# A two-layer decoder trunk on one core: half of the last output projection by seven block products instead of eight, and the last scan begun sooner

## The chip, the cores and the metric

The kernel runs on one core of a Trainium2 chip. The metric is the device time of one execution in microseconds; before the change the median of 3 runs is 2236.33 us (2235.79 to 2238.73). Lower is better.

## The reference

One sequence of 512 tokens, 2048 channels, two residual layers in f32: layer 0 is gated differential attention, layer 1 gated RWKV-7 time mixing. The change concerns layer 1, and there the last scan and the output projection:

```python
D_MODEL = 2048
SEQ = 512
DEPTH = 2

def wkv7_scan(r, w, k, v, a, b):
    ...
    def step(S, inp):
        r_t, w_t, k_t, v_t, a_t, b_t = inp
        sa = jnp.einsum('bhvk,bhk->bhv', S, a_t)
        S = S * w_t[:, :, None, :] + sa[..., None] * b_t[:, :, None, :] + v_t[..., None] * k_t[:, :, None, :]
        y = jnp.einsum('bhvk,bhk->bhv', S, r_t)
        return S, y

def rwkv7_mixer(...):
    ...
    y = wkv7_scan(rh, heads(decay), kh, vh, -kk, kk * ah)
    mean = jnp.mean(y, axis=-1, keepdims=True)
    var = jnp.mean(jnp.square(y - mean), axis=-1, keepdims=True)
    y = (y - mean) * lax.rsqrt(var + GN_EPS)
    y = y * gn_w.astype(F32).reshape(RW_HEADS, RW_HEAD_DIM) + gn_b.astype(F32).reshape(RW_HEADS, RW_HEAD_DIM)
    y = y + jnp.sum(rh * kh * r_k.astype(F32), axis=-1, keepdims=True) * vh
    ...
```

The gated y (512 x 2048) is multiplied with w_out (2048 x 2048), and the product is added to the residual x.

## The kernel before

**Arithmetic.** Every large f32 product is made of three fast ones (`mm3`): each operand is split into a high part, rounded to the fast format (fp32r), and a low part, the rest. ACT makes the high part with a copy, DVE the low part with a subtraction; for weights `split_w` (L96, L97) does so from a raw buffer that SP's queue loads (`load_w`, L78). Buffers in SBUF: `wraw` three, `wh` two, `wl` two. The split runs with a high priority (`urgent`, AHEAD = 2000), scan steps with a higher one (SCAN = 3000): a scheduler orders each engine's instructions by priority and by when they can go, and each engine then works through its own list in that order.

**Layer 1.** It goes through 16 pairs of heads (j). For each pair come four projections of 128 channels, keys and queries, a small triangular solve on DVE (`t_solve`, ends in the store td<-Tm), which comes back through a transfer (TT<-td, issued by SP) and is turned on DVE (L874). Then a chain of small PE steps, inserted between the products of other work: `t_combine` (L880, L890), then the scan over 8 blocks of tokens with three small PE operations each (L961, L972, L979) that go through ACT, DVE and POOL, then `outputs` (L1001, L1005). `Chain` counts the products that `mm3` issues (`tick`): the three numbers in `chain(g, j, p, delay, gap, gap_s)` say how many products lie before the chain's first PE step (beginning with T's turn on DVE) and between its later ones. For the pairs 0 to 13 the gated y goes to DRAM (`yd2`, [2048, 512], channel by token); for the pairs 14 and 15 it is split in SBUF.

**The last scan.** For pair 15 nothing follows but the gate projections of pairs 13, 14 and 15 and the output projection, so its chain, with 80, 4, 4, is laid between those products. `split_rows` loads rows 0 to 13 of yd2 back and splits them; rows 14 and 15 come straight from `gated(..., True)`.

**The output projection.** Four quarters (`cb`) of 512 columns. In each, `unit_tok` goes over 8 units of two k-tiles (a unit is 256 weight rows, 512 KB) and, in each, over 4 token tiles: 2 x 4 x 3 = 24 products of 128x128 by 512 into four PSUM tiles (two `pp`, two `pt`). y is the stationary operand, the weights are streamed. In the first quarter the last unit goes k-tile by k-tile, as row 15 comes last (`all_rows`). Then for each token tile the residual row (`xr1`, loaded by SP from xd) is added on DVE (L1126) and stored through ACT's queue (L1127).

**The lines that the prediction speaks of**: L96 and L97 (split of weights), L108 (every product), L407 and L408 (split of a row of y), L874, L880, L890 (T of the solve), L1005 (end of a scan), L1125 to L1127 (residual, sum, store). The tile tags AR, G, BK, BKT, LT, VS, y, yc, r, k, th0, th1, xL, xH, E, f, l name buffers that earlier stages of layer 1 use.

Of the kernel before, what the change touches and what calls it, by code (L numbers as in the profile page):

```python
# [13 lines left out]
F32 = mybir.dt.float32  # L14
F32R = mybir.dt.float32r
# [3 lines left out]
ALU = mybir.AluOpType  # L19
# [4 lines left out]
P = 128  # L24
# [14 lines left out]
AHEAD, SCAN, SOLVE = 2000, 3000, 4000  # L39
# [45 lines left out]

@urgent
def split_w(g, parts, kg, cols, k0, raw=None, fine=False):

    nc = g.nc
    if raw is None:  # L90
        raw = g.wraw.tile([P, kg, cols], F32, name="wraw", tag="wraw")
        load_w(g, raw, parts, k0, slice(0, kg))
    hi = g.wh.tile([P, kg, cols], F32R, name="wh", tag="wh")
    lo = g.wl.tile([P, kg, cols], F32R, name="wl", tag="wl")
    for ks in [slice(k, k + 1) for k in range(kg)] if fine else [slice(0, kg)]:
        nc.scalar.copy(hi[:, ks], raw[:, ks])  # L96
        nc.vector.tensor_sub(lo[:, ks], raw[:, ks], hi[:, ks].bitcast(F32))  # L97
    return hi, lo
# [4 lines left out]
    return [(win, h * 256, 256), (win, D + h * 256, 256)]  # L103


def mm3(nc, out, aH, aL, bH, bL, start, stop, g=None):
    for a, b, s, e in ((aH, bH, start, False), (aH, bL, False, False), (aL, bH, False, stop)):
        m = nc.tensor.matmul(out, a, b, start=s, stop=e)  # L108
        if g:
            tick(g, m)  # L110
    return m
# [26 lines left out]
def tick(g, m):  # L138

    g.m = m  # L140
    if g.chains:
        c = g.chains[0]
        c.wait -= 1
        if c.wait <= 0:
            with g.tc.issue_after(m.ins):
                c.step(g)


def unit_tok(g, aH, aL, parts, cols, npp=NT, more=None):
# [473 lines left out]
@urgent  # L623
def shift_mix(g, ps, rows, mu, omu, tag, bufs=2):

    nc, w = g.nc, g.work
    o_ = w.tile([P, T], F32, name="mix" + tag, tag=tag, bufs=bufs)
    nc.scalar.activation(o_[:rows, :], ps[:rows, :], AF.Copy, scale=omu)
    nc.vector.scalar_tensor_tensor(o_[:rows, 1:], ps[:rows, 0 : T - 1], mu, o_[:rows, 1:], ALU.mult, ALU.add)  # L629
    return o_  # L630
# [310 lines left out]
def chain(g, j, p, delay, gap, gap_s, others=()):  # L941
    def steps():
        yield from t_combine(g, j, p)
        yield from scan_pair(g, j, p, gap, gap_s, dict(others))

    p.chain = Chain(g, steps(), delay)
    return p.chain
# [93 lines left out]
    nc.vector.scalar_tensor_tensor(p.y[:], ps[:], g.prm["hgw"][:, j : j + 1], p.y[:], ALU.mult, ALU.add)  # L1041


def layer1(g, aps):
    nc, tc = g.nc, g.tc
    with ExitStack() as cx:
        g.lc = cx.enter_context(tc.tile_pool(name="lc1", bufs=1))
        g.work = cx.enter_context(tc.tile_pool(name="work1", bufs=2))
        rwkv_masks(g)
        w = g.work  # L1050
        win = aps["rw_w_in"][0]
        pairs = []

        def proj(i, j, **k):
            return unit_chan(g, [(win, i * D + j * P, P)], P, **k)[0]

# [48 lines left out]
        gated(g, j - 2, pairs[j - 2], gate(g, j - 2, proj(3, j - 2)))  # L1105
        gps = proj(3, j - 1)
        group_norm(g, j - 1, pairs[j - 1])
        finish_y(g, j - 1, pairs[j - 1])
        row = gated(g, j - 1, pairs[j - 1], gate(g, j - 1, gps), True)
        gt = gate(g, j, proj(3, j))  # L1110
        rows = split_rows(g, g.yd2, ("r", "k", "th0", "th1"), 1, j - 1) + [row]

        def all_rows(n, _):
            if n >= KT and len(rows) < KT:
                group_norm(g, j, p)
                finish_y(g, j, p)
                rows.append(gated(g, j, p, gt, True))

        yH, yL = Rows(rows, 0), Rows(rows, 1)
        for cb in range(4):  # L1120
            cs = slice(cb * 512, (cb + 1) * 512)
            pts = unit_tok(g, yH, yL, [(aps["rw_w_out"][0], cb * 512, 512)], 512, 2, more=all_rows)
            for t in range(NT):
                xr = w.tile([P, 512], F32, name="xr1", tag=("r", "k", "th0", "th1")[t], bufs=1)
                nc.sync.dma_start(out=xr[:], in_=g.xd[t * P : (t + 1) * P, cs])  # L1125
                nc.vector.tensor_add(xr[:], xr[:], pts[t][:])  # L1126
# [48 lines left out]
```

## Time and profile before

| | |
|---|---|
| median of 3 runs | 2236.33 us (2235.79 to 2238.73) |
| the profiled execution | 2235.41 us |
| its span | 2233.7 us |
| DMA packets in all | 224.46 MB, mean 100 GB/s |
| end of the last scan on PE (L1005) | 2077.39 us + 0.68 |
| last product begins | 2229.34 us |

The profile is one execution. PE is the matrix engine (PEld its weight loads), DVE the vector engine, ACT the scalar engine, POOL the general one, SP the engine that issues most DMAs. A row of a group reads: line, engine, operation, tiles out<-in, shape, count, then busy us and mean ns of one, then the idle time ahead of them and what ended it. A row of a timeline reads: start, duration, engine, line, operation, and in brackets the idle time before. PE's records overlap: a product's record is 0.39 us long, and the next one begins 0.23 later. PEclk is the clock that PE was granted, 1.00 for full.

### The profile page before, as it was taken

What the parts mean: (1) busy time and instruction counts of PE and PEld (TensorE: products, weight loads), DVE (VectorE), ACT (ScalarE), POOL (GpSimd) and SP (SyncE); (2) the same over time, 40 slices, a digit from 0 to 9 for tenths busy, and PEclk for the clock granted to TensorE, in tenths of its full rate; (3) what the DMA queues carried; (4) which work ended last, traced back from release to release, by engine and by line L of the source; (5) the groups of instructions that cost most, each with busy time, mean ns of one, the idle gap of its engine ahead of it and who ended that gap; (6) DMA issues with size and microseconds to landing.
All of it is one profiled execution on the core that took longest, in us unless ns stands there. A gap on an engine that the chain in (4) does not pass through costs nothing. (4 is left out here: it accounts for less than half of the span.)

```text
span 2233.7 us, 33774 instructions
## 1 busy us (share of the span) xinstructions
PE 2184.1 (98%) x12260; PEld 1770.4 (79%) x12260; DVE 1374.9 (62%) x3666; ACT 1005.1 (45%) x2065; POOL 297.4 (13%) x672
## 2 busy tenths in 40 slices
PE   8999999999999999989999999999999999999999
PEld 6888888888888878877777777787777777777887
DVE  5555646455564664245667787777777877777322
ACT  5443434334343452225455555555455556545211
POOL 0000000000000000000323133333322233331000
PEclk9999999999999999999999999999999999999999
DMA  6222222222222254332423333333333333435333
GB/s 180 94 86 96 85 95 95 85 95 85 95 85 95 91 194 132 115 113 74 102 68 83 88 88 86 86 91 99 90 81 81 97 88 78 107 93 156 123 132 113
DMA packets 290730, 224.46 MB, mean 100 GB/s; under 512 B 47732, under 2 KB 255748, under 8 KB 290564
## 3 DMA queue, kind: packets, MB, share of 16 engines
q1 hardware_dynamic: 275892, 195.74, 30.2%
q0 software_dynamic: 6144, 10.84, 2.0%
q10 hardware_dynamic: 8528, 15.73, 2.0%
q8 instruction: 96, 1.57, 0.3%
q14 instruction: 70, 0.57, 0.1%
HBM read 202.26 MB, written 19.99 MB: 99 GB/s over the span
## 5 line engine op out<-in xcount | busy, mean ns | idle before, releaser
L97 DVE TENSOR_TENSOR wl<-wraw,wh 128x1024 fp32r<-128x1024 f32 (+2 forms) x325 | 396.0, 1219 | 498.8 <-ACT wh L96 498.2
L96 ACT CAST wh<-wraw 128x1024 fp32r<-128x1024 f32 (+2 forms) x325 | 340.0, 1046 | 659.1 <-PE pp L108 453.9
L108 PE MATMUL pp<-wh,hH 128*128 128x512 f32 x1408 | 554.7, 394 | 6.0 <-ACT hH L586 5.3
L108 PE MATMUL pp<-wh,hL 128*128 128x512 f32 x1408 | 552.6, 393 | 0.0
L108 PE MATMUL pp<-wl,hH 128*128 128x512 f32 x1408 | 552.0, 392 | 0.0
L108 PE MATMUL pp<-hL,wh 128*128 128x512 f32 (+1 forms) x1056 | 430.3, 407 | 0.1
L108 PE MATMUL pp<-hH,wl 128*128 128x512 f32 (+1 forms) x1056 | 428.3, 406 | 0.4 <-DVE wl L97 0.4
L108 PE MATMUL pp<-hH,wh 128*128 128x512 f32 (+1 forms) x1056 | 425.1, 403 | 2.1 <-DVE mixt L629 1.8
L108 PEld LDWEIGHTS pp<-wh,hH 128*128 128x128 f32 x1408 | 265.1, 188 | 60.2 <-ACT hH L586 6.0
L108 PEld LDWEIGHTS pp<-wh,hL 128*128 128x128 f32 x1408 | 265.0, 188 | 54.2 <-DVE hL L587 0.6
L108 PEld LDWEIGHTS pp<-wl,hH 128*128 128x128 f32 x1408 | 265.2, 188 | 52.3
L108 PEld LDWEIGHTS pp<-hH,wh 128*128 128x128 f32 (+1 forms) x1056 | 199.4, 189 | 40.6 <-DVE mixt L629 2.2
L108 PEld LDWEIGHTS pp<-hL,wh 128*128 128x128 f32 (+1 forms) x1056 | 199.4, 189 | 37.5 <-DVE hL L587 1.7
L108 PEld LDWEIGHTS pp<-hH,wl 128*128 128x128 f32 (+1 forms) x1056 | 199.6, 189 | 34.0 <-DVE wl L97 0.8
L850 DVE SCALAR_TENSOR_TENSOR tmpl<-LT,Tm 128x60 f32<-128x60 f32 (+24 forms) x496 | 133.1, 268 | 10.7
L967 POOL COPY SA<-VS 64x64 f32<-64x64 f32 x224 | 58.0, 259 | 445.6 <-DVE VS L983 388.1
L678 POOL MEMSET rmask<- 128x512 bf16 x1 | 0.5, 525 | 832.9 <-DVE nb L339 832.9
L852 DVE TENSOR_TENSOR Tm<-Tm,tmpl 128x60 f32<-128x60 f32 (+24 forms) x496 | 104.6, 211 | 10.9
L983 DVE SCALAR_TENSOR_TENSOR VS<-sm,gam,Sg 64x64 f32<-64x64 f32 x192 | 54.3, 283 | 51.9 <-PE sm L979 47.6
L964 ACT COPY rhs<-sm 64x64 f32<-64x64 f32 x256 | 52.6, 205 | 66.7 <-PE sm L961 64.4
L974 ACT COPY VS<-sm 64x64 f32<-64x64 f32 x256 | 52.6, 206 | 59.0 <-PE sm L972 55.2
L970 POOL TENSOR_SCALAR Sg<-SA,gam 128x64 f32<-128x64 f32 x96 | 72.1, 751 | 9.3
(269 smaller groups left out, 2801.3 us busy)
## 6 DMA issues: line engine op xcount, KB each, us to landing
wraw<-in_rw_w_in_dram SPq DMA_DIRECT2D x128, 512.0 KB, 4.0
wraw<-in_da_w_in_dram SPq DMA_DIRECT2D x254, 256.0 KB, 3.0
wraw<-in_da_w_out_dram SPq DMA_DIRECT2D x32, 512.0 KB, 3.6
wraw<-in_rw_w_out_dram SPq DMA_DIRECT2D x32, 512.0 KB, 3.6
LT<-ltd POOLq DMA_DIRECT2D x64, 132.0 KB, 2.9
yr<-yd SPq DMA_DIRECT2D x28, 256.0 KB, 3.8
xq<-in_x_dram SPq DMA_DIRECT2D x16, 256.0 KB, 5.2
xd<-xq ACTq DMA_DIRECT2D x16, 256.0 KB, 2.9
```

Source lines behind the costliest of these rows:

```text
L96: nc.scalar.copy(hi[:, ks], raw[:, ks])
L97: nc.vector.tensor_sub(lo[:, ks], raw[:, ks], hi[:, ks].bitcast(F32))
L108: m = nc.tensor.matmul(out, a, b, start=s, stop=e)
L678: nc.gpsimd.memset(g.rmask[:], 1.0)
L850: nc.vector.scalar_tensor_tensor(tt, LT[:, i : i + 1, i + 1 :].to_broadcast([P, s, n]), n2[:, i : i + 1], Tm[:, 0:s, i : i + 1].to_broadca ...
L852: nc.vector.tensor_add(Tm[:, 0:s, i + 1 :], Tm[:, 0:s, i + 1 :], tt)
L964: nc.scalar.copy(rhs[r_, :], sm[r_, h * C : h * C + C])
L967: nc.gpsimd.tensor_copy(p.SA[r_, c - 1, :], VS[r_, c, h, :])
L970: nc.gpsimd.tensor_scalar(Sg[:], p.SA[:, c - 1, :], p.gam[:, c : c + 1], None, ALU.mult)
L974: nc.scalar.copy(VS[r_, c, h, :], sm[r_, P : P + C])
L983: g.state = nc.vector.scalar_tensor_tensor(VS[r_, c + 1, h, :], s_, p.gam[r_, c : c + 1], Sg[r_, :], ALU.mult, ALU.add)
```

## The change

Three things change, all in layer 1.

1. The last scan's chain gets 24, 5, 6 in place of 80, 4, 4.
2. The first two quarters go as before. During the second, `all_sums` issues `sum_forms` four times, within units 0, 1, 3 and 5 (counted from 0): it reloads 14 rows of yd2 (k-tiles 0 to 6 and 7 to 13, in chunks of 1, 2, 2 and 2 tiles of each half) into raw buffers (`frow`, tag wraw), and makes four sums of quarter blocks (256 tokens by 7 k-tiles) on DVE, split by ACT and DVE into buffers that are free by then. The residual tiles of the second quarter use the AR buffers, two token tiles in each.
3. The last 1024 columns, two blocks c1 and c2 of 512, are made by `half_out`: y's tokens (two halves of 256), k-tiles 0 to 13 (two halves of seven) and the columns (c1, c2) form a 2x2 by 2x2 block product with the seven products of Winograd's form; k-tiles 14 and 15 are multiplied in full (`plain`). The weight sums (`comb`) are made on DVE from raw tiles, b11 is loaded twice, the outputs are gathered in f32 in four `acc` tiles that start from the residual (`take`), and stored from there.

```diff
-def mm3(nc, out, aH, aL, bH, bL, start, stop, g=None):
+def mm3(nc, out, aH, aL, bH, bL, start, stop, g=None, skip=False):
...
+NS = 7
+KS = ((0, 1), (1, 2), (3, 2), (5, 2))
+PLACES = {"11": (0, 0), "12": (0, 1), "21": (1, 0), "22": (1, 1)}
...
+def sum_forms(g, src, i):
+    nc, w = g.nc, g.work
+    k0, n = KS[i]
+    rows, out, wide = [], {}, []
+    for at in (k0, NS + k0):
+        r = g.wraw.tile([P, n, 512], F32, name="frow", tag="wraw")
+        nc.sync.dma_start(out=r[:], in_=src[at * P : (at + n) * P, :].rearrange("(k p) t -> p k t", p=P))
+        rows.append(r)
+    (a, b), (c, d) = [(r[:, :, 0:256], r[:, :, 256:512]) for r in rows]
+    for nm, o, x, y, op in (("S1", d, b, d, ALU.add), ("S3", b, a, b, ALU.subtract), ("S2", d, d, a, ALU.subtract),
+                            ("S4", c, c, d, ALU.subtract)):
+        nc.vector.tensor_tensor(out=o, in0=x, in1=y, op=op)
...
+        nc.scalar.copy(hi, o)
+        nc.vector.tensor_sub(lo, o, hi.bitcast(F32))
+        out[nm] = hi, lo
+    return out
...
+def half_out(g, w, dst, sums, rows, cb):
+    nc, wk = g.nc, g.work
+    c1, c2 = cb * 1024, cb * 1024 + 512
+    X = [g.pp.tile([P, 512], F32, name="pp", tag="pp") for _ in range(2)]
+    Y = lambda tag="pb": [g.ps.tile([P, 512], F32, name="pt", tag=tag, bufs=2) for _ in range(2)]
+    acc = {}
+    for nm in ("11", "22", "12", "21"):
+        t, c = PLACES[nm]
+        acc[nm] = wk.tile([P, 2, 512], F32, name="acc", tag="AR", bufs=3)
+        nc.sync.dma_start(out=acc[nm][:], in_=g.xd[t * 256 : t * 256 + 256, (c1, c2)[c] : (c1, c2)[c] + 512].rearrange(
+            "(t p) c -> p t c", p=P))
+    T01 = wk.tile([P, 3, 512], F32, name="T01", tag="G1", bufs=2)
+    Ts = [T01[:, 0:1], T01[:, 1:3], wk.tile([P, 2, 512], F32, name="T2", tag="BK", bufs=1)[:],
+          wk.tile([P, 2, 512], F32, name="T3", tag="LT", bufs=1)[:]]
...
+    def split(raw, n):
+        return split_w(g, None, n, 512, 0, raw)
+
+    def prod(out, i, form, wt, first, end):
+        k0, n = KS[i]
+        wh, wl = split(wt, n)
+        for k in range(n):
+            for t in range(2):
...
+                mm3(nc, out[t][:], a[0], a[1], wh[:, k, :], wl[:, k, :], first and k == 0, end and k == n - 1, g, True)
...
+    def take(nm, ps):
+        with g.tc.high_priority(offset=SCAN):
+            for t in range(2):
+                nc.vector.tensor_add(acc[nm][:, t, :], acc[nm][:, t, :], ps[t][:])
...
+    def comb(o, a, b):
+        with g.tc.high_priority(offset=AHEAD):
+            nc.vector.tensor_sub(o, a, b)
+
+    N = len(KS)
+    y = Y()
+    for i, (k0, n) in enumerate(KS):
+        b11 = load(k0, n, c1)
+        prod(X, i, "11", b11, i == 0, i == N - 1)
+        b12 = load(k0, n, c2)
+        comb(Ts[i], b12[:], b11[:])
+        prod(y, i, "S1", Ts[i], i == 0, i == N - 1)
+    take("11", X)
+    take("22", y)
+    b22 = []
+    for i in (0, 2):
+        for a in (i, i + 1):
+            b22.append(load(NS + KS[a][0], KS[a][1], c2))
+            comb(Ts[a], b22[a][:], Ts[a])
+            prod(X, a, "S2", Ts[a], False, a == N - 1)
+        if i == 2:
+            take("12", X)
+        for a in (i, i + 1):
+            prod(y, a, "S4", b22[a], False, False)
+    wt = split(load(2 * NS, 2, c2), 2)
+    plain(y, 0, wt, False)
+    take("12", y)
+    store("12")
+    z = Y("pc")
+    plain(z, 2, wt, True)
+    take("22", z)
+    for i, (k0, n) in enumerate(KS):
+        b11 = load(k0, n, c1)
+        comb(b11[:], Ts[i], b11[:])
+        prod(X, i, "S3", b11, False, i == N - 1)
+    take("22", X)
+    store("22")
+    y = Y()
+    b21 = []
+
+    def second(i):
+        b21.append(load(NS + KS[i][0], KS[i][1], c1))
+        comb(Ts[i], b21[i][:], Ts[i])
+        prod(y, i, "12", b21[i], i == 0, False)
+
+    def fourth(i):
+        prod(X, i, "22", Ts[i], False, False)
+
+    for f, i in ((second, 0), (second, 1), (fourth, 0), (fourth, 1), (second, 2), (fourth, 2)):
+        f(i)
+    b21.append(load(NS + KS[3][0], KS[3][1], c1))
+    comb(Ts[3], b21[3][:], Ts[3])
+    fourth(3)
+    wt = split(load(2 * NS, 2, c1), 2)
+    plain(X, 2, wt, False)
+    take("21", X)
+    store("21")
+    prod(y, 3, "12", b21[3], False, False)
+    plain(y, 0, wt, False)
+    take("11", y)
+    store("11")
...
-        chain(g, j, p, 80, 4, 4)
+        chain(g, j, p, 24, 5, 6)
...
-        for cb in range(4):
+        for cb in range(2):
             cs = slice(cb * 512, (cb + 1) * 512)
-            pts = unit_tok(g, yH, yL, [(aps["rw_w_out"][0], cb * 512, 512)], 512, 2, more=all_rows)
+            pts = unit_tok(g, yH, yL, [(aps["rw_w_out"][0], cb * 512, 512)], 512, 2, more=(all_rows, all_sums)[cb])
             for t in range(NT):
-                xr = w.tile([P, 512], F32, name="xr1", tag=("r", "k", "th0", "th1")[t], bufs=1)
+                if not cb:
+                    xr = w.tile([P, 512], F32, name="xr1", tag=("r", "k", "th0", "th1")[t], bufs=1)
+                elif t % 2 == 0:
+                    xr = wide = w.tile([P, 2, 512], F32, name="xr1", tag="AR", bufs=3)
+                xr = wide[:, t % 2, :] if cb else xr
                 nc.sync.dma_start(out=xr[:], in_=g.xd[t * P : (t + 1) * P, cs])
                 nc.vector.tensor_add(xr[:], xr[:], pts[t][:])
                 nc.scalar.dma_start(out=aps["out"][t * P : (t + 1) * P, cs], in_=xr[:])
+        half_out(g, aps["rw_w_out"][0], aps["out"], sums, rows, 1)
```

More of the change, by code (lines that the diff above doesn't have):

```diff
@@ L103, in qk_cols @@
     return [(win, h * 256, 256), (win, D + h * 256, 256)]
-def mm3(nc, out, aH, aL, bH, bL, start, stop, g=None):
+def mm3(nc, out, aH, aL, bH, bL, start, stop, g=None, skip=False):
     for a, b, s, e in ((aH, bH, start, False), (aH, bL, False, False), (aL, bH, False, stop)):
-        m = nc.tensor.matmul(out, a, b, start=s, stop=e)
+        m = nc.tensor.matmul(out, a, b, start=s, stop=e, skip_group_check=skip)
         if g:
@@ L1041, in finish_y @@
     nc.vector.scalar_tensor_tensor(p.y[:], ps[:], g.prm["hgw"][:, j : j + 1], p.y[:], ALU.mult, ALU.add)
+NS = 7
+KS = ((0, 1), (1, 2), (3, 2), (5, 2))
+PLACES = {"11": (0, 0), "12": (0, 1), "21": (1, 0), "22": (1, 1)}
+SUM_TAGS = ({"S1": "l", "S2": "E", "S4": "f", "S3": "xH"},
[3 rows of a table added]
+SUM_BUFS = {"BKT": 2, "VS": 2, "G1": 2, "y": 4}
+def sum_forms(g, src, i):
[10 more added lines that the diff above has]
+        nc.vector.tensor_tensor(out=o, in0=x, in1=y, op=op)
+        tag = SUM_TAGS[i][nm]
+        one = lambda shape, t: w.tile(shape, F32R, name="f" + nm, tag=t, bufs=SUM_BUFS.get(t, 1))
+        if isinstance(tag, tuple):
+            hi, lo = [one([P, n, 256], t)[:] for t in tag]
+        elif tag == "G1":
+            if not wide:
+                wide.append(one([P, 2, 2, n, 256], tag))
+            hi, lo = [wide[0][:, int(nm[1]) - 1, x] for x in range(2)]
+        else:
+            both = one([P, 2, n, 256], tag)
+            hi, lo = both[:, 0], both[:, 1]
+        nc.scalar.copy(hi, o)
+        nc.vector.tensor_sub(lo, o, hi.bitcast(F32))
+        out[nm] = hi, lo
+    return out
@@ new lines, in half_out, with load, plain, store @@
+def half_out(g, w, dst, sums, rows, cb):
[12 more added lines that the diff above has]
+          wk.tile([P, 2, 512], F32, name="T3", tag="LT", bufs=1)[:]]
+    def load(k0, n, c):
+        raw = g.wraw.tile([P, n, 512], F32, name="wraw", tag="wraw")
+        load_w(g, raw, [(w, c, 512)], k0, slice(0, n))
+        return raw
+    def split(raw, n):
[5 more added lines that the diff above has]
+            for t in range(2):
+                s = slice(t * P, (t + 1) * P)
+                if form in PLACES:
+                    half, kb = PLACES[form]
+                    at = slice(half * 256 + t * P, half * 256 + (t + 1) * P)
+                    a = [x[:, at] for x in rows[kb * NS + k0 + k]]
+                else:
+                    a = [x[:, k, s] for x in sums[i][form]]
+                mm3(nc, out[t][:], a[0], a[1], wh[:, k, :], wl[:, k, :], first and k == 0, end and k == n - 1, g, True)
+    def plain(out, t0, wt, first):
+        for k, (yH, yL) in enumerate(rows[2 * NS :]):
+            for t in range(2):
+                s = slice((t0 + t) * P, (t0 + t + 1) * P)
+                mm3(nc, out[t][:], yH[:, s], yL[:, s], wt[0][:, k, :], wt[1][:, k, :], first and k == 0,
+                    k == 1, g, True)
+    def take(nm, ps):
+        with g.tc.high_priority(offset=SCAN):
+            for t in range(2):
+                nc.vector.tensor_add(acc[nm][:, t, :], acc[nm][:, t, :], ps[t][:])
+    def store(nm):
+        t, c = PLACES[nm]
+        for i in range(2):
+            r0 = (2 * t + i) * P
+            nc.scalar.dma_start(out=dst[r0 : r0 + P, (c1, c2)[c] : (c1, c2)[c] + 512], in_=acc[nm][:, i, :])
+    def comb(o, a, b):
[55 more added lines that the diff above has]
+    store("11")
```

4 lines of the change are left out of this document (added), and 3 rows, old and new, of the table SUM_TAGS.

## The prediction

> **What bounds the kernel now.** I read the page first: busy times, then the chain that ended last.
>
> ```profile
> span 2233.7 us, 33774 instructions
> PE 2184.1 (98%) x12260; PEld 1770.4 (79%) x12260; DVE 1374.9 (62%) x3666; ACT 1005.1 (45%) x2065; POOL 297.4 (13%) x672
> PE 11%; DVE 2%; issue 0%; ACT 0%; DMA 0%; SPq 0%; ACTq 0%; DVEq 0%
> ```
>
> PE is busy for 98% of the span, and the chain followed back from the end is almost all PE. Next the stretches of the tail, where the change lies (columns: the stretch, its length, busy us of PE, PEld, DVE, ACT, POOL, granted clock, DMA share, GB/s), and the chain in order of time:
>
> ```profile
> 2050.00:2080.00 30.00, 29.49 (x190) 21.31 (x189) 14.04 (x29) 13.47 (x39) 7.61 (x20) 1.00 0.43 138
> 2080.00:2230.00 150.00, 149.73 (x663) 123.66 (x661) 47.67 (x59) 28.59 (x28) 0.00 (x0) 1.00 0.37 125
> ```
>
> ```profile
> 2104.61 2.72 PE pp L108 x12
> 2107.33 2.72 PE pt L108 x12
> ...
> 2224.29 1.36 PE pp L108 x6
> 2225.65 1.36 PE pt L108 x6
> ```
>
> PE never waits there at all: 12 products take 2.72 us, so 0.2267 us each, and DVE is busy for a third of the time. A product removed from this stretch is worth 0.2267 us, as long as nothing new makes PE wait. So the question is only whether the supply of the operands keeps up.
>
> **What it removes.** Over the last 1024 columns the old code issues 2 x 16 k-tiles x 4 token tiles x 3 = 384 products. The new one issues seven block products of 7 x 2 x 3 = 42, and k-tiles 14 and 15 in full, 2 x 2 x 4 x 3 = 48: 342. **Removed: 42 x 0.2267 = 9.52 us.** Shapes stay 128x128 by 512 columns.
>
> **What it adds beside PE.** The costs of one operation, by shape:
>
> ```profile
> L97 DVE TENSOR_TENSOR wl<-wraw,wh 128x1024 fp32r<-128x1024 f32 x35 | 42.9, 1225 | 97.9 <-ACT wh L96 97.9
> L96 ACT CAST wh<-wraw 128x1024 fp32r<-128x1024 f32 x35 | 36.9, 1053 | 119.0 <-PE pt L108 94.5 <-DVE xr L1126 13.2 <-PE pp L108 11.2
> L408 DVE TENSOR_TENSOR hL<-yr,hH 128x512 fp32r<-128x512 f32 x14 | 9.2, 690 | 2.1 <-ACT hH L407 2.0
> L407 ACT CAST hH<-yr 128x512 fp32r<-128x512 f32 x14 | 8.1, 617 | 1.4 <-DMA yr<-yd 1.3
> ```
>
> No f32 sum of two loaded tiles of 128x1024 shows before; the nearest row is the split's subtraction, 1.22, and its half 0.69, and I take them. The sums for the second quarter are four chunks of eight DVE operations, 8 x 0.69 = 5.5 us (the one-tile chunk less), at most 22 us in a quarter of 43.5 us (192 x 0.2267), in which DVE had about 14 (47.67 of 150, times 43.5). DVE has room. In the last half the weight differences (4 x 0.69 + 12 x 1.22 = 17.4), 30 splits (7 x 0.69 + 23 x 1.22 = 32.9) and eight takes of 1.38 (11) are 61 us in about 78: room again, but DVE works in order, and its order decides the waits below.
>
> **Wait of the short units.** wh and wl have two buffers, so the cast for a unit begins when the unit two before it is done:
>
> ```profile
> 2104.70 1.05 ACT L96 CAST wh<-wraw 128x1024 fp32r<-128x1024 f32 x1 [4.39 <-PE pt L108]
> 2105.78 1.23 DVE L97 TENSOR_TENSOR wl<-wraw,wh 128x1024 fp32r<-128x1024 f32 x1 [4.21 <-ACT wh L96]
> ```
>
> The unit before begins at 2104.61, and wl is whole at 2107.01, 2.40 us on. Today a unit is 24 products (5.44 us), which hides that, and a new unit of 12 (2.72) just does. A unit of 6 lasts 1.36, and the next one needs wl with its second product, at 1.59: a wait of 0.8. That is so behind four units of one k-tile (products S2, S4, 12 and 22 of chunk 0): **4 x 0.8 = 3.2 us**; from 0.4 each (if the cast is let go earlier) to 1.3 (a take or a difference ahead of the split on DVE).
>
> **Wait at the first product of the last half.** Raw weights have three buffers, and the loads take:
>
> ```profile
> wraw<-in_rw_w_out_dram SPq DMA_DIRECT2D x32, 512.0 KB, 3.6
> yr<-yd SPq DMA_DIRECT2D x28, 256.0 KB, 3.8
> xr<-xd SPq DMA_DIRECT2D x12, 256.0 KB, 5.3
> ```
>
> In the changed order of DVE, the difference for the third chunk stands ahead of the split for the first S1 product, and the loads form a chain. From the end of the split of the second quarter's last unit but one: the loads of b11 and b12 (0.6 apart, 3.6) 4.2, their difference 0.69, the last unit's split 1.23, which frees a buffer, b12 of the next chunk 3.6, difference 1.23, b12 of the third chunk 3.6, difference 1.23, and only then the split 0.69: 16.5. PE has at that moment 5.44 - 2.40 = 3.04 of a unit, two units, six products and one: 3.04 + 10.88 + 1.36 + 0.23 = 15.5. So 1.0 if the second quarter's splits are on time, 0.6 with loads 0.15 shorter each. They are hardly on time: two units (10.88 us) now send four tiles through the three raw buffers, two weights held 3.6 + 1.05 + 1.23 = 5.9 each, two reloads held 3.8 + 5 x 0.69 = 7.3 and 3.8 + 8 x 0.69 = 9.3, 28.4 in all, 9.5 us of three buffers' time. That leaves no more than a tenth, and a slip may eat the 3.04 of slack before PE sees it, so the wait can be up to 4.0. I take **2.5**, nearer to the late end.
>
> **Wait where b11 is loaded again (S3).** DVE's order has the difference of S3's second tile ahead of the split of its first, and that of the fourth ahead of the split of the second. From the end of the split of the last S4 unit: load 3.6, difference 1.22, split 0.69 (frees a buffer), load 3.6, difference 1.22, a take 0.69, split 1.22: 12.2. PE meanwhile has 2.72 - 2.40, three units of 2.72, six products and one: 0.32 + 8.16 + 1.36 + 0.23 = 10.1. **2.1 us**; 1.5 with loads of 3.3, 5.5 with loads of 5.3.
>
> **The scan begun sooner.**
>
> ```profile
> 2013.94 0.68 PE L1005 MATMUL Y<-SA,AR 64*64 64x64 f32 x28
> 2014.55 0.50 PE L108 MATMUL pp<-hH,wl 128*128 128x512 f32 x1
> ...
> 2037.46 1.09 PE L880 MATMUL px<-T,G 32*32 32x32 f32 x32
> ```
>
> ```profile
> 2029.11 0.43 DVE L874 STREAM_TRANSPOSE T<-TT 64x256 f32<-64x256 f32 x1
> 2030.17 0.44 DVE L874 STREAM_TRANSPOSE T<-TT 64x256 f32<-64x256 f32 x1 [0.63 <-DMA TT<-td]
> ```
>
> The solve's T is whole at 2029.54 (first head) and 2030.61, and nothing ahead of it changes. In the changed order 62 products stand between L1005 and L880, so PE is there at 2014.6 + 62 x 0.2267 = 2028.7 and **waits 0.9**; everything behind it on PE waits along, the second head (five products later, 2030.9) no more. The wider gaps between the scan's steps can save what PE idled in them, 0.5 at most by the first stretch above (30.00 - 29.49); I take 0.4. Sum **+0.5**, bounds 0 and +1.4. The last scan's result is ready sooner, but the last row of y was in time already, so that gives nothing.
>
> Costed at nothing: the residual tiles of the second quarter now use the AR buffers and their loads stand earlier in SP's queue, behind the loads of T. They wait for L1005 of the last scan but one, 2013.94 + 0.68, and stand behind a transfer issued later than that, so neither they nor the weights behind them are held; if that cover were gone, a weight load (3.6) would be late. The 14 reloads read rows stored before the last row of y is made. At the end there are two stores where four were: at most 0.3 less.
>
> **The clock.** Two waits of 2 to 3 us are new for this tail, and this is what such waits did elsewhere (third number from the right in the stretches: granted clock):
>
> ```profile
> 1117.33 0.69 PE L880 MATMUL px<-T,G 32*32 32x32 f32 x16 [2.28 <-DVE T L874]
> ...
> 1669.98 0.46 PE L961 MATMUL sm<-VS,G 128*128 128x128 f32 x2 [2.94 <-DVE VS L986]
> ...
> 1671.42 0.63 PE L108 MATMUL pp<-hH,wh 128*128 128x512 f32 x1
> 1671.85 0.63 PE L108 MATMUL pp<-hL,wh 128*128 128x512 f32 x1
> ...
> 1034.77 0.50 PE L108 MATMUL pp<-hH,wh 128*128 128x512 f32 x1 [1.75 <-DVE mixt L629]
> ```
>
> ```profile
> 1033.00:1036.00 3.00, 1.25 (x6) 1.00 0.03 8
> ...
> 1118.00:1121.00 3.00, 3.00 (x21) 0.50 1.10 248
> ...
> 1672.00:1674.00 2.00, 2.00 (x8) 0.50 0.25 55
> ```
>
> After an idle of 2.94 the clock fell to half, and products started 0.43 apart instead of 0.2267; after 2.28 it fell too, after 1.75 not. A fall that lasts 3.4 us costs 3.4 / 0.43 = 8 products of 0.2 more: **1.6 us**. I count one such fall for the two waits. The Trainium skill ("TensorE: Matmul & The Clock Gate", Why this matters for your kernels) says to leave no idle of PE over about 3 us, and its Part 1 gives a free-running window of 3413 ns; the row at 2.28 us says that less is enough here. By that rule no wait above would make the clock fall, and the sum would be 1.6 less.
>
> **Sum.** -9.5 + 3.2 + 2.5 + 2.1 + 0.5 + 1.6 = **+0.4**. The profiled execution took 2235.41 (span 2233.7 and 1.7 around it), so 2235.8; it stands 0.9 under the median of the runs shown, 2236.33, so **2236.7**. Within 0.2% (4.5 us, about what a measurement of this kernel can tell from no change) is 2231.9 to 2240.8.
>
> **The rivals.**
> 1. The same waits, but the clock stays up: 2235.1. For it, the idle of 1.75 without a fall; against it, that of 2.28. The Trainium skill's rule cited above gives this time too.
> 2. The supply keeps up, and the waits take their lower ends, 4 x 0.4, 0.6 and 1.5, 0 for the scan, no fall: -9.5 + 3.7 = -5.8, so **2230.5**. For it: the median load is 3.6 us, DVE and ACT have half their time free, and DMA carries 125 GB/s of what bursts show as 270 (below). Against it: the chains above are in order on one engine and hold no slack.
> 3. **Slower: the three raw buffers become the bound.** The ring of the second quarter has 32.6 us of buffer time for two units, of which 28.4 - 2 x 3.6 - 2 x 3.8 = 13.6 isn't loading: it decides from a mean load of (32.6 - 13.6) / 4 = 4.75 us on. Loads beside others take longer:
>
> ```profile
> 2187.00:2196.00 9.00, 9.00 (x41) 7.47 (x40) 2.45 (x2) 1.40 (x2) 0.00 (x0) 1.00 0.85 270
> 2196.00:2226.00 30.00, 30.00 (x134) 24.83 (x133) 6.12 (x5) 5.28 (x5) 0.00 (x0) 1.00 0.14 49
> ```
>
> The second quarter must now carry 4.2 MB of weights, 3.7 of reloads and 1.05 of output in 43.5 us, 206 GB/s throughout and in bursts, near the crowded stretch, in which loads took the 5.3 us above. At 5.3 the ring takes (13.6 + 21.2) / 3 = 11.6 a chunk, 0.7 over, 2.9 for four, and the last two loads of the chain at the half's start, beside 1 MB of residual tiles and the stores, 1.7 each: 0.4 + 2.9 + 3.4 = +6.7, so **2243.0**. Against it: 3.8 us is the median of reloads of the same size.
> 4. The sooner scan does no more than move a wait: that is in the sum, and alone, without the seven products, it would give 2236.3 + 0.5.
>
> **How the numbers follow.** The forecast has 0.28 and rival 1 0.17, both within 0.2%; rival 2 0.24, faster; rival 3 0.31, slower. The range, 2230.5 to 2244, goes from rival 2 to a little over rival 3; the likeliest one's own is 2233 to 2240.5.
>
> **What would show it.** Right: 42 products fewer in the tail; L880 of the last scan idle by about 0.9 for T; an idle of 2 to 3 us early in the last half that ends with a split (wl), one of about 2 where b11 comes again, four of 0.8, and a half clock behind one of the first two. Wrong: waits for wl in the second quarter (rival 3), loads over 4.7 us there, or idle times in the last half that sum to under 4 us (rival 2). A difference from before outside the tail, or DVE slower in the sums than 0.69 and 1.22, would break the working itself.

## The result, and the profile after

The changed kernel takes **2248.19 us** (median of 4 runs, 2246.76 to 2249.1) against 2236.06 for the kernel before in the same runs: a ratio of 1.0055, 95% interval 1.0037 to 1.0072. It is slower, by 12 us, and above the predicted range (2230.5 to 2244). Every ratio is to the kernel before in the same rounds, whose median was 2235.1 to 2237.6 us there, so ratios compare better than times do.

The profiled execution of the changed kernel took 2246.76 us. First the page: span, busy times, the chain that ended last by engine.

```profile
span 2244.8 us, 33824 instructions
PE 2182.7 (97%) x12218; PEld 1764.5 (79%) x12218; DVE 1425.4 (63%) x3736; ACT 1024.9 (46%) x2095; POOL 299.2 (13%) x672
PE 8%; DVE 3%; DMA 2%; ACT 1%; issue 1%; POOL 0%; DVEq 0%; SPq 0%; ACTq 0%; POOLq 0%
```

42 products fewer are there (12260 to 12218), but the span grew by 11.1 us, and DMA and ACT, 0% of the last chain before, now have a part in it. Where it went is read from the stretches. For both kernels I take the second quarter (from its first product to the first one of the last half) and the last half up to the end of its last product; the columns are as in the prediction. Before:

```profile
2099.01:2142.53 43.52, 43.52 (x193) 36.04 (x192) 12.53 (x13) 8.44 (x8) 0.00 (x0) 1.00 0.43 145
2142.53:2229.57 87.04, 87.04 (x385) 71.88 (x383) 23.83 (x24) 15.82 (x15) 0.00 (x0) 1.00 0.37 122
```

After:

```profile
2099.05:2149.49 50.44, 46.19 (x193) 36.74 (x192) 28.93 (x39) 14.92 (x20) 0.00 (x0) 0.97 0.56 187
2149.49:2240.85 91.36, 83.84 (x342) 64.09 (x342) 56.85 (x61) 27.66 (x29) 0.00 (x0) 0.98 0.41 136
```

The second quarter begins at the same time in both (2099.01 and 2099.05), so by these two profiles nothing came from the scan; the runs below test it. The same 192 products then take **6.9 us more**, and the last half, with 42 products fewer, **4.3 us more**: 91.36 where 342 x 0.2267 = 77.5 would do, so 13.8 us of waits and of half clock there. With 0.1 less behind the last product these make up the 11.1.

In the second quarter, the chain that sets the end in order of time:

```profile
2107.37 2.73 PE pt L108 x12
2110.12 1.05 ACT wh L96
2111.19 1.22 DVE wl L97
2112.41 0.61 DVE fS L1081
2113.04 5.56 DMA frow<-yd
...
2118.72 0.70 DVE frow L1068
2119.45 0.70 DVE frow L1068
2120.17 0.63 ACT fS L1080
2120.83 0.69 DVE fS L1081
2121.52 0.61 DVE frow L1068
...
2122.76 1.22 DVE wl L97
2123.98 1.21 DVE fS L1081 x2
2125.21 4.98 DMA frow<-yd
...
2142.19 5.25 DMA wraw<-in_rw_w_out_dram
2147.53 1.23 DVE T L1145
```

This is a loop. The second reload of a chunk (frow) must land, then come the sums in turn between DVE and ACT, with a weight split among them, and the last of them frees the raw buffer into which the second reload of the next chunk goes. One round, from load to load, takes 2125.21 - 2113.04 = 12.2 us, and PE works through the two units of a chunk in 10.9. What the round starts with is a reload of 5 to 5.6 us; the first one even took 7.3, issued at 2098.70 among the four stores of the first quarter, and that round took 14.3. What DMA and SP's queue show (the first view: issues with KB each and median us to landing, from 2097 to 2140; the second, from 2099 to 2150: what SP waited for, in total, times, longest):

```profile
frow<-yd SPq DMA_DIRECT2D x6, 512.0 KB, 5.3
wraw<-in_rw_w_out_dram SPq DMA_DIRECT2D x6, 512.0 KB, 3.6
out_dram<-xr ACTq DMA_DIRECT2D x4, 256.0 KB, 6.6
```

```profile
SPq L78 <- DVE frow L1068: 16.9, 3, 7.0
SPq L78 <- DVE wl L97: 10.9, 6, 2.4
```

Weight loads (L78) waited 16.9 us in all for sums (L1068) to give a buffer back. PE's end of it:

```profile
2111.21 0.50 PE L108 MATMUL pp<-wh,hH 128*128 128x512 f32 x1 [1.12 <-ACT wh L96]
2112.47 0.79 PE L108 MATMUL pp<-wl,hH 128*128 128x512 f32 x1 [0.76 <-DVE wl L97]
...
2149.49 0.47 PE L108 MATMUL pp<-wh,hH 128*128 128x512 f32 x1 [1.77 <-DVE xr L1298]
...
2154.80 0.50 PE L108 MATMUL pt<-wl,fS 128*128 128x512 f32 x1 [2.97 <-DVE wl L97]
...
2204.44 0.80 PE L108 MATMUL pp<-wl,fS 128*128 128x512 f32 x1 [2.17 <-DVE wl L97]
```

The first two and the third are most of the second quarter's loss. The third, at the end of the quarter, is one of order on DVE too: PE needs a PSUM tile that the residual sum (xr) frees, and that sum stands behind the weight difference for the second chunk (2147.53, the last line of the chain above), whose load took 5.25. The last two are the waits that the prediction expected at the first S1 product and at S3. DVE's timeline at these two:

```profile
2152.92 1.23 DVE L1145 TENSOR_TENSOR T<-wraw 128x1024 f32<-128x1024 f32 x1 [1.77 <-DMA wraw<-in_rw_w_out_dram]
2154.06 0.69 DVE L97 TENSOR_TENSOR wl<-T,wh 128x512 fp32r<-128x512 f32 x1
...
2201.43 1.22 DVE L1145 TENSOR_TENSOR wraw<-T,wraw 128x1024 f32<-128x1024 f32 x1 [1.04 <-DMA wraw<-in_rw_w_out_dram]
2202.57 0.68 DVE L1135 TENSOR_TENSOR acc<-acc,pt 128x512 f32<-128x512 f32 x1
2203.17 2.35 DVE L97 TENSOR_TENSOR wl<-wraw,wh 128x1024 fp32r<-128x1024 f32 x2
```

Both times DVE sat before a difference (at S1 that for the third chunk, at S3 that for the fourth) until its load landed, and the split that PE needed came after it.

### The profile page after: what moved, and what is told of

Its sections match the earlier page's. It is cut to its first block, busy times and chain, and to the rows that moved or that the text cites. A ratio compares the mean times of both kernels' runs of the same rounds, so it can differ in the third digit from the quotient of the medians.

```text
span 2244.8 us, 33824 instructions
## 1 busy us (share of the span) xinstructions
PE 2182.7 (97%) x12218; PEld 1764.5 (79%) x12218; DVE 1425.4 (63%) x3736; ACT 1024.9 (46%) x2095; POOL 299.2 (13%) x672
## 5 line engine op out<-in xcount | busy, mean ns | idle before, releaser
L108 PE MATMUL pp<-wh,hH 128*128 128x512 f32 x1376 | 542.6, 395 | 9.7 <-ACT hH L586 6.0
L108 PE MATMUL pp<-wl,hH 128*128 128x512 f32 x1376 | 541.3, 393 | 1.4 <-DVE wl L97 1.4
L108 PE MATMUL pp<-wh,hL 128*128 128x512 f32 x1376 | 540.8, 393 | 0.0
L108 PEld LDWEIGHTS pp<-wh,hH 128*128 128x128 f32 x1376 | 259.4, 189 | 64.9 <-ACT hH L586 6.6
L108 PEld LDWEIGHTS pp<-wl,hH 128*128 128x128 f32 x1376 | 259.6, 189 | 53.9 <-DVE wl L97 2.7
L108 PEld LDWEIGHTS pp<-wh,hL 128*128 128x128 f32 x1376 | 259.5, 189 | 52.7 <-DVE hL L587 0.6
L852 DVE TENSOR_TENSOR Tm<-Tm,tmpl 128x60 f32<-128x60 f32 (+24 forms) x496 | 104.4, 210 | 10.9
```

Source lines behind the costliest of these rows:

```text
L108: m = nc.tensor.matmul(out, a, b, start=s, stop=e, skip_group_check=skip)
L852: nc.vector.tensor_add(Tm[:, 0:s, i + 1 :], Tm[:, 0:s, i + 1 :], tt)
```

## The experiments

Twelve kernels, in three groups. "Second quarter" and "last half" are the two stretches above, taken in each kernel's own profile, which is one execution.

### Is it the scan?

```diff
-        chain(g, j, p, 24, 5, 6)
+        chain(g, j, p, 80, 4, 4)
```

> The changed kernel with the last scan's chain put back to 80, 4, 4 and all else kept. In the profile of the change the second quarter of the output projection begins at 2099.05 us, before the change at 2099.01: by that the sooner scan gave nothing. Theory: this kernel takes what the changed one takes, 2248 us within 2. Rival: the sooner scan is what lets the reloads and the accumulators' loads start where they collide, and without it the second quarter is shorter: 2244 or less; or it did give something that a later wait took back, and this is slower by 2 us or more.

Measured: 2248.23 us, ratio 1.0044 (1.0031 to 1.0056); second quarter 49.47, last half 90.41. And the same edit the other way, alone in the kernel before:

> The kernel before with only the last scan's chain begun sooner (24, 5, 6). Theory: the wait of about 0.9 us for T ahead of L880 is paid and about as much idle time between the scan's steps is saved: 2236 us within 1.5. Rival: the sooner scan takes 2 us or more off by itself, so the seven products cost more than the 12 us that show.

Measured: 2237.84 us, ratio 1.0002 (0.9987 to 1.0017); second quarter 43.52, last half 87.04. Both theories hold, the second against the kernel before in its own rounds (2237.6): the sooner scan neither costs nor gives what can be told, which is some 3 us, and the loss lies in the second quarter and the last half. (The wait at L880 is there, 0.79 us idle in the changed kernel and 1.58 in this one; the second quarter begins at 2099.05 and 2099.50 all the same.)

### Is it the bytes or the buffers?

```diff
-    for at in (k0, NS + k0):
-        r = g.wraw.tile([P, n, 512], F32, name="frow", tag="wraw")
+    for at, tag in ((k0, "BK"), (NS + k0, "LT")):
+        r = w.tile([P, n, 512], F32, name="frow", tag=tag, bufs=1)
```

> The changed kernel with the reloaded rows in two tiles of their own (tags BK and LT, free at that time) instead of in the three raw weight buffers; the same bytes, the same sums. Theory (ring): the 6.9 us that the second quarter lost (50.45 us from its first product to the next block's first, before 43.52), and part of the 3.1 us ahead of the first S1 product, came from a late reload holding back a weight load: here the second quarter takes 44 to 45 us, the S1 wait falls to about 1 to 2, and the time is 2239 to 2242. Rival (bytes): the loads are slow because 8.9 MB pass in that quarter, whatever buffers they go to: the second quarter stays at 48 us or more and the time at 2246 or more.

Measured: 2241.78 us, ratio 1.0015 (1.0001 to 1.003), where the changed kernel has 1.0055. The two stretches, and in the second quarter the loads:

```profile
2102.84:2146.36 43.52, 43.52 (x194) 36.04 (x192) 23.66 (x31) 12.77 (x16) 0.00 (x0) 1.00 0.46 152
2146.36:2237.40 91.04, 84.89 (x343) 65.11 (x341) 56.21 (x60) 27.66 (x29) 0.00 (x0) 0.96 0.40 137
```

```profile
wraw<-in_rw_w_out_dram SPq DMA_DIRECT2D x8, 512.0 KB, 3.9
out_dram<-xr ACTq DMA_DIRECT2D x4, 256.0 KB, 4.6
frow<-yd SPq DMA_DIRECT2D x2, 512.0 KB, 5.4
```

PE has no wait at all in the second quarter, though the reloads that fall into it take as long as before (5.4). But two of the chunks are reloaded and summed earlier here, during the last scan, since they no longer wait for a raw buffer, and the third is reloaded by then (DVE is busy for 28.9 us of the changed kernel's quarter, 23.7 here). So bytes, sums and buffers are not told apart yet. The last half kept its length, and of its 13.5 us over 77.5 two falls of the clock are 3.2. The next kernel has the rows in the same tiles, but no reload before the last row of y:

```diff
+        if not i:
+            nc.vector.tensor_copy(r[:, 0, 0:1], g.late[:, 0:1].bitcast(F32))
         nc.sync.dma_start(out=r[:], in_=src[at * P : (at + n) * P, :].rearrange("(k p) t -> p k t", p=P))
...
+                g.late = rows[KT - 1][1]
                 sums.append(sum_forms(g, g.yd2, len(sums)))
```

> The changed kernel with the reloaded rows in tiles of their own, as in the kernel that took 2241.78 us, but the first chunk's tiles get one element from the last row of y before they are loaded, so that no reload can begin before the second quarter is about to: there, two chunks had been reloaded and summed during the last scan already, which took bytes and sums out of the quarter, too. Here all 3.7 MB and all sums are in it. Theory (ring): only the sharing of the three raw buffers costs time there; the second quarter takes 43.5 to 45 us and the whole 2240 to 2244. Rival (bytes and sums): what helped was that half of the reloads came earlier; the second quarter is at 47 us or more and the time at 2245 or more.

Measured: 2240.75 us, ratio 1.0028 (1.0016 to 1.004). Its two stretches, and the reloads of 512 KB:

```profile
2099.26:2143.55 44.29, 43.68 (x194) 35.88 (x192) 30.32 (x45) 15.91 (x23) 0.00 (x0) 1.00 0.53 181
2143.55:2237.75 94.20, 86.36 (x342) 65.87 (x342) 56.79 (x61) 27.70 (x29) 0.00 (x0) 0.95 0.40 137
```

```profile
frow<-yd SPq DMA_DIRECT2D x6, 512.0 KB, 4.4
```

All the sums (30.3 us of DVE) and nearly as many bytes a second as in the changed kernel (181 GB/s to 187) are in the quarter, and it takes 44.3 us, 0.77 over the bare products. But its last half takes 94.2, 2.8 more than in the changed kernel: near its beginning PE waited 4.2 us for the split of b11's second tile, which stood on DVE behind a difference, and this behind its load; two windows of half clock followed. The load, a line of the chain that ended last (start, duration):

```profile
2142.83 6.23 DMA wraw<-in_rw_w_out_dram
```

So a part of what the second quarter gained is lost again behind it: the two stretches together are 3.3 us shorter than in the changed kernel, those of the kernel with early reloads 7.2. And the opposite, shared buffers without the load:

```diff
-        nc.sync.dma_start(out=r[:], in_=src[at * P : (at + n) * P, :].rearrange("(k p) t -> p k t", p=P))
+        nc.gpsimd.memset(r[:], 0.5)
```

> The changed kernel with the reloads left out: each raw buffer for rows is filled with a constant by POOL in place of the load, so the sums, and with them the output, are those of a constant. The three raw buffers are still shared and all sums are made. Theory (ring with slow loads): the round from one chunk's second row tile to the next is the reload (5 to 5.6 us) and 6.6 us of sums; with a fill of some 1 to 2 us in place of the reload it is 8 to 9, less than PE's 10.9, and the second quarter takes 43.5 to 45 us. Rival (order of the sums on DVE and ACT): the splits of weights stand behind the sums whatever these waited for, and the quarter stays at 47 us or more.

Measured: 2240.08 us, ratio 1.0017 (1.0005 to 1.0028); second quarter 43.52, by this row of it, with the same 28.5 us of DVE; the fill takes 0.96 us a tile:

```profile
2104.86:2148.38 43.52, 43.52 (x193) 36.04 (x192) 28.45 (x39) 15.06 (x20) 3.82 (x4) 1.00 0.39 137
```

So it takes both, the reloads' time and the three buffers that they share with the weights. With either one taken away, the second quarter is within 0.8 us of its bare products: in that quarter the bytes alone cost no more than that, and the order of the sums on DVE and ACT costs nothing. (What late reloads cost behind the quarter rests on one profile of each kernel: 94.20 against 91.04, one more window of half clock included.)

### The short units, and the order on DVE

To the kernel with rows in tiles of their own:

```diff
-        return split_w(g, None, n, 512, 0, raw)
+        return split_w(g, None, n, 512, 0, raw, True)
```

> As the kernel with rows in tiles of their own, and each weight unit of the last half split one k-tile at a time (cast and subtraction of 128x512 twice instead of 128x1024 once). Theory: a short unit's successor then needs 0.1 + 0.62 + 0.69 = 1.4 us from the start of the unit before, less than the 1.6 it has, so the waits of 0.4 to 0.6 behind units of six products go, and the wait at S3 falls by about 1.5: 3 to 5 us faster than without, 2235 to 2238. Rival: DVE and ACT work longer (1.38 against 1.23 and 1.24 against 1.05 for a unit) and DVE's order stays, so what is gained at short units is lost in the long chains: within 1 us of the kernel without.

Measured: 2234.38 us, ratio 0.9986 (0.9974 to 0.9998): faster than the kernel before by 0.14%, with an interval that ends just short of 1. The last half takes 84.33, 6.7 less; two falls of the clock (3.2) no longer happen, and the rest, 3.5, are the short units (of seven waits of 0.33 to 0.45 behind units of six products two are left, and two of 0.2 to 0.3 are new) and shorter waits at S1 (0.45 + 1.69 from 0.88 + 1.84) and S3 (1.23 from 2.49). The same edit with the reloads still in the raw buffers:

> The changed kernel with only the splits of the last half made one k-tile at a time; the reloads stay in the raw weight buffers. Theory: the two faults are separate and add: the second quarter still loses 6 to 7 us to the ring (50 us instead of 43.5), the last half loses about as little as with rows in tiles of their own (85 to 87 us instead of 91.35), and the time is 2241 to 2244. Rival: a late ring makes the last half start behind, so that the finer split finds nothing to save at its start: last half 89 us or more, 2246 or more.

Measured: 2242.43 us, ratio 1.003 (1.0016 to 1.0045); second quarter 50.88, last half 86.40. The two faults are separate and add, as the theory had it: 0.0025 of the ratio goes with the fine split, 0.0040 with the rows' own tiles, 0.0069 with both.

Then the long waits. First by giving PE more to do ahead of them:

```diff
-    for i, (k0, n) in enumerate(KS):
-        b11 = load(k0, n, c1)
-        prod(X, i, "11", b11, i == 0, i == N - 1)
-        b12 = load(k0, n, c2)
-        comb(Ts[i], b12[:], b11[:])
-        prod(y, i, "S1", Ts[i], i == 0, i == N - 1)
+    for i in (0, 2):
+        for a in (i, i + 1):
+            k0, n = KS[a]
+            b11 = load(k0, n, c1)
+            prod(X, a, "11", b11, a == 0, a == N - 1)
+            b12 = load(k0, n, c2)
+            comb(Ts[a], b12[:], b11[:])
+        for a in (i, i + 1):
+            prod(y, a, "S1", Ts[a], a == 0, a == N - 1)
```

> Rows in tiles of their own, fine splits, and in the first phase of the last half the products go 11, 11, S1, S1 for two chunks at a time instead of 11, S1 in turn. Without this, the first S1 product waited 1.9 us from product to product (split behind the difference for the third chunk). Theory (order on DVE): PE now has 18 products ahead of the first S1 one instead of 6, 2.7 us more, so that wait goes below 0.5, and the last half takes 82 to 83 us instead of 84.3: 2232 to 2234. Rival: the wait is for loads through three raw buffers, which b11 and b12 of two chunks now fill for longer: it reappears at the second pair, and the last half stays at 84 or more.

Measured: 2234.35 us, ratio 0.9997 (0.9986 to 1.0009); last half 85.85. A miss: a wait of 1.53 now stands at the split of b11's second tile, which DVE does behind the same difference, and one fall of the clock followed it.

```diff
-    for i, (k0, n) in enumerate(KS):
+    for i in (1, 2, 3, 0):
+        k0, n = KS[i]
         b11 = load(k0, n, c1)
         comb(b11[:], Ts[i], b11[:])
-        prod(X, i, "S3", b11, False, i == N - 1)
+        prod(X, i, "S3", b11, False, i == 0)
```

> As the one with products in pairs, and the S3 products go over chunks 1, 2, 3, 0 instead of 0, 1, 2, 3, so that the phase begins with a unit of 12 products instead of one of 6. The wait there was 1.46 us from product to product. Theory: PE has 1.36 us more to do while the load and the difference of the fourth chunk stand ahead of the split on DVE, so the wait falls to 0.3 or less, and the last half takes 1.0 to 1.3 us less than with pairs alone. Rival: the load goes out later by as much, because the buffer it needs is freed by a unit of twice the length; no gain.

Measured: 2232.24 us, ratio 0.9999 (0.9985 to 1.0013); last half 84.94. Against pairs alone that is 0.9 less, but pairs alone had a fall of the clock there (1.6). The wait at S3's start is gone, and two others, of 1.89 and 1.22 from product to product, came behind it in the phase after. A miss as well, and by the ratio no gain. The same with the scan at 80, 4, 4:

> As the one with pairs and S3 reordered, but with the last scan's chain at 80, 4, 4. Theory: the sooner scan waits 0.9 to 1.6 us for T at L880 and saves nothing that the second quarter needs, so this is equal to the sooner one within 1 us, or up to 1 us faster. Rival: the sooner scan frees the buffers for the sums and the rows early enough, and without it the first reloads come late: 2 us or more slower.

Measured: 2233.72 us, ratio 0.9999 (0.9987 to 1.001); last half 84.57. Once more no difference by the scan.

Then by changing the order on DVE itself (`g.sub` is the last subtraction of a split; `subs` collects them for S1, `subs3` for S3, where the same is done):

```diff
-    def comb(o, a, b):
-        with g.tc.high_priority(offset=AHEAD):
+    def comb(o, a, b, after=None):
+        with g.tc.issue_after(after.ins) if after else ExitStack(), g.tc.high_priority(offset=AHEAD):
             nc.vector.tensor_sub(o, a, b)
...
-        comb(Ts[i], b12[:], b11[:])
+        comb(Ts[i], b12[:], b11[:], subs[i - 2] if i > 1 else None)
         prod(y, i, "S1", Ts[i], i == 0, i == N - 1)
+        subs.append(g.sub)
...
-        comb(b11[:], Ts[i], b11[:])
+        comb(b11[:], Ts[i], b11[:], subs3[i - 2] if i > 1 else None)
```

Alone in the changed kernel:

> The changed kernel with only the order of DVE altered in two phases: the weight difference of chunk i is placed behind the split for chunk i - 2 of S1 and of S3, where it stood ahead of it. Reloads stay in the raw buffers, splits stay whole. Theory (order on DVE): the wait at the first S1 product (3.1 us) falls to 1 or less and that at S3 (2.3) to about 1, and the last half takes 87 to 89 us instead of 91.35; the second quarter stays at about 50 us; 2244 to 2246. Rival: these waits are for loads that the ring makes late, the split is no sooner and the waits stay or come back one unit later: 2247 or more.

Measured: 2244.84 us, ratio 1.0033 (1.0022 to 1.0045); second quarter 48.95, last half 88.95, with no fall of the clock in it where the changed kernel had one (1.6). The wait at the first S1 product is gone, but 2.15 us stand at the second tile of b11 instead; at S3 0.70 are left of 2.33, and 1.50 came later. So the time agrees with the theory and the mechanism does so only in part: without the finer split and with the full ring most of the wait moves one unit on. With rows in tiles of their own and fine splits:

> Rows in tiles of their own, fine splits, and the differences of S1 and S3 behind the split two chunks earlier. Theory: the last half's two long waits that are left (1.9 us at S1 and 1.46 at S3, from product to product) fall below 0.5 each, the last half takes 81.5 to 82.5 us instead of 84.3, and the time is 2231.5 to 2233.5, faster than the kernel before by about 0.15%. Rival: as with the products in pairs, the wait reappears at the next unit, which needs the load or difference that was put back: 84 us or more, 2234 or more.

Measured: **2233.62 us, ratio 0.9981 (0.9969 to 0.9993)**, faster than the kernel before. The waits at the first S1 product and at S3 are gone, and part of the rival came true: 1.39 from product to product now stand at the second tile of b11. Its two stretches, and that wait, the longest left in the last half:

```profile
2100.69:2144.21 43.52, 43.52 (x194) 36.05 (x193) 23.67 (x31) 12.67 (x16) 0.00 (x0) 1.00 0.46 152
2144.21:2225.41 81.20, 79.84 (x343) 63.54 (x341) 58.16 (x83) 30.01 (x52) 0.00 (x0) 1.00 0.46 153
```

```profile
2148.82 0.50 PE L108 MATMUL pp<-wl,hH 128*128 128x512 f32 x1 [1.23 <-DVE wl L97]
```

The last half is 3.7 us over the bare products, where the changed kernel had 13.8, and the clock stays at 1.00 throughout. Of the 3.7, 1.85 are waits (1.39, 0.24 and 0.22). Over 1 us more is no wait at all: products whose stationary operand is one of the sums (fS) start a little further apart than those on y. Between these two lie 12 starts, so 0.2333 each in place of 0.2267:

```profile
2174.17 0.39 PE L108 MATMUL pp<-wl,fS 128*128 128x512 f32 x1
...
2176.97 0.39 PE L108 MATMUL pp<-wl,fS 128*128 128x512 f32 x1
```

Over the 168 products on sums that makes 1.1 us, in the changed kernel as well; why they are slower is open. The last half is 5.8 us shorter than the 87.04 of before, and the ratio (4.2 us, interval 1.6 to 6.9) agrees with that.

## Why the prediction was wrong

**What failed** is one step: "no more than a tenth" of slack in the ring of the second quarter, costed at nothing in the sum. It added up how long each tile holds a raw buffer (28.4 of 32.6 us) and took that for a bound. The loads measured 5.3 for reloads and 3.6 for weights, a mean of 4.45, so with these loads in that count the ring should still have kept up, its limit being 4.75. It did not: the tiles don't share the buffers freely. The second reload of a chunk goes into the buffer that the sums of the chunk before give back last, and that loop has a length of its own, 12.2 us for 10.9 of PE. The 9.3 us that the count gave that tile (3.8 of load, eight sums of 0.69) were 12.2: load 5 to 5.6, and 6.6 for the sums, as they wait for ACT's copies and for a weight split. The other tiles were held longer, too: in the round from 2113.04 the four have a buffer for 12.2, 9.7, 8.3 and 6.0 us, from the issue of the load to the end of the last user, and that is 36.2 of the 36.5 that three buffers have.

The term that was 0 measured **6.9**: 3.1 of waits within the quarter, 1.9 at its end, behind the difference on DVE, and most of the rest a fall of the clock (1.6). The fall isn't what it takes: the same quarter took 49.47, 50.88 and 48.95 in the profiles of the scan at 80, of the fine split alone and of the order on DVE alone, without one. Rival 3, which had the largest chance (0.31), had the place and the sign, with 2.9 for the quarter by a crowded load, and its 2243.0 came nearest. No run has a fourth raw buffer, which would test the ring by itself.

**The short units**: 4 x 0.8 = 3.2 were forecast. Seven waits of 0.33 to 0.44 from product to product stand in the profile behind units of six products, 2.7 in all. Each is half of the 0.8 that was forecast, near its lower bound of 0.4, and there are nearly twice as many: that the total comes close is luck.

**S1**: 2.5 forecast, up to 4.0; measured 3.37 - 0.23 = 3.1 from product to product, by the order on DVE that was named (the timeline above). The reason given for taking more than 1.0, late splits of the second quarter, was not it: with the quarter on time at 43.52, 0.88 + 1.84 are still lost there with rows in tiles of their own, and 0.88 + 2.87 in the kernel without reloads. Not foreseen was another 1.0 at the third chunk's S1, behind the difference for the fourth, whose load took 6.1 us behind two accumulator tiles of 512 KB.

**S3**: 2.1 forecast, 2.33 measured, by the order that was named (the same timeline).

**The scan**: a wait of 0.9 at L880 was forecast and 0.95 measured (1.18 from product to product, less 0.23). The gain was taken at 0.4. The two profiles have the second quarter begin at the same time, so it would be about as large as the wait and the sum 0 instead of +0.5; the two experiments can't tell these apart, as their intervals are some 3 us to either side.

**The clock**: one fall for two waits in the last half, as forecast, and one more in the second quarter.

**What no term held**: these sizes with the removed 9.5 make 8.1 of the 11.1 by which the profile grew. The other 3.0 lie in the last half: 1.1 for the slower products on sums, about 1.2 for the one or two products behind each wait, which start some 0.1 late (2154.80 and 2155.14 at S1, 0.34 apart), and small differences of start.

**Rival 2** (the supply keeps up) is what the kernel comes near to with its faults removed: 81.20 us of the last half are 3.7 over the bare products, and rival 2 had 3.7 for its waits. That the two numbers are equal is chance, as only 1.85 of the measured ones are waits, and those in other places.

## What to carry to other kernels

Don't ask of a buffer ring only whether its capacity suffices: follow one buffer round (load, each user in the order of its engine, release, next load) with the loads that a crowded stretch shows, and hold that loop against the time that the consumer takes; when two streams share the buffers, a late tile of the one holds the other back. Here two tiles of a stage that was over could take one of the streams, at no cost in memory. Where an engine works in order, look at what stands ahead of the operation that PE waits for: more work ahead of PE only moved such a wait, while a finer split and another order on that engine, together and with the ring mended, took away most of it.

## What was not expected of the hardware

The length of an idle time doesn't say whether the clock falls. In the changed kernel 2.97 us of idle PE went by without, and 2.17 did not. The falls of this profile begin on a grid: between those of the tail, 2112.30 and 2204.46, lie 92.16 us, which is 27.0 times 3.413. Windows of that grid (columns as above, busy us of PE second, granted clock third from the right):

```profile
2108.89:2112.30 3.41, 1.70 (x7) 0.84 (x5) 3.12 (x5) 2.09 (x3) 0.00 (x0) 1.00 0.41 127
2112.30:2115.71 3.41, 3.24 (x8) 2.57 (x9) 1.94 (x3) 1.04 (x1) 0.00 (x0) 0.50 0.62 199
2146.44:2149.85 3.41, 1.64 (x8) 1.08 (x7) 2.32 (x3) 0.00 (x0) 0.00 (x0) 1.00 0.31 118
2149.85:2153.26 3.41, 1.98 (x8) 1.00 (x6) 1.64 (x4) 1.67 (x2) 0.00 (x0) 1.00 0.95 298
2153.26:2156.67 3.41, 1.87 (x8) 1.57 (x9) 2.62 (x3) 0.64 (x1) 0.00 (x0) 1.00 0.79 264
2201.05:2204.46 3.41, 1.24 (x6) 0.53 (x5) 3.03 (x4) 1.48 (x2) 0.00 (x0) 1.00 0.35 120
2204.46:2207.87 3.41, 3.41 (x8) 2.73 (x9) 1.48 (x2) 0.00 (x0) 0.00 (x0) 0.50 0.82 252
```

A window in which PE was busy for 1.70 or 1.24 of 3.41 us was followed by one at half clock; two with 1.98 and 1.87, between which the idle 2.97 us were divided, were not. But the window just ahead of these two, with only 1.64, was not followed by a fall either, so PE's busy share of one such window doesn't decide by itself; what does stays open. The Trainium skill ("TensorE: Matmul & The Clock Gate", Part 1) gives a free-running window of 3413 ns, and the trace agrees with that. Under "Why this matters for your kernels" the same page of the Trainium skill advises against idle times of PE over about 3 us, which is too wide here, as 2.17 us that fall into one window were enough.
